# Five accumulation tiles and three tiles for transposes, instead of six and two, in layer 1's query, key and value stage

## The chip, the cores and the metric

One core of a Trainium2 chip runs the whole program. The metric is the device time of one execution in microseconds, the median of three runs. A profile of one further execution gives the time line of each engine: TensorE (PE; its weight loads are listed as PEld), VectorE (DVE), ScalarE (ACT), GpSimd (POOL) and the DMA queue that SyncE (SP) issues.

## What is computed

The reference is a model of two layers over 2048 tokens and 256 context tokens of width 1024, in float32. Layer 0 is a mixer of convolutions and a state space scan; layer 1 is attention with low-rank projections, 16 heads and a query and key width of 96 (64 without and 32 with rotary positions). The change lies in the part that makes layer 1's queries, keys and values:

```
cq, ckv, kr, gate = jnp.split(h @ w_in, cuts, axis=-1)          # widths 384, 256, 32, 1024
q  = (rms_norm(cq, q_a_norm) @ w_uq).reshape(b_, n, 16, 96)
kv = (rms_norm(ckv, kv_a_norm) @ w_ukv).reshape(b_, n, 16, 64 + 64)
q_nope, q_rope = rms_norm(q[..., :64], ...), rms_norm(q[..., 64:], ...)
k_nope, v, k_rope = rms_norm(kv[..., :64], ...), kv[..., 64:], rms_norm(kr, ...)
q_rope, k_rope = apply_rope(q_rope, cos, sin), apply_rope(k_rope, cos, sin)
```

## The kernel before

Float32 products are made in float32 precision from three matmuls (high by high, high by low, low by high; lines 120 to 122 in `mm3`). The stage works on 18 tiles of 128 tokens: tiles 0 and 1 are context (no queries), 2 to 17 are the tokens. For each tile there are these steps, and the names below are those of the code:

- `b_in(n)`: the down projection, one PSUM tile `pk` (288 columns, 24 matmuls) and one `pq` (384 columns, 24 matmuls). ScalarE squares both for the norms (L1382 to L1388).
- `b_r3(n)`: the three reciprocal square roots of a tile, a chain of small VectorE operations (L1397, L1398, L127 to L135).
- `b_cn(n)`: scales and writes the normed row `cn`; it is the last reader of `pk` and `pq` (ScalarE L1405 and L1410, VectorE L1407).
- `b_tr(n)`: two tiles of transposes of `cn` (L1430 to L1448).
- `b_up(n)`: four accumulation tiles for keys and values (512 columns, 6 matmuls each, L1468 to L1470 empty them, the last reader is VectorE's L1470) and four for queries (384 columns, 9 matmuls each, emptied by ScalarE's L1498), then the norms of all heads on VectorE (`k_scale`, the chain rB) and the scaling on GpSimd (L1483, L1509 to L1521).
- `b_heads(n)`: five tiles of four transposes (`evacT`, L1527), each emptied by ScalarE (L1541 or L1538) and then VectorE (L1542 or L1539) and stored by a DMA.

All accumulation tiles come from one PSUM pool (`accB`) and all transposes from another (`tpB`); together the two pools hold eight tiles. A buffer is handed out again once the last instruction that reads it is done, so a later tile's first matmul waits for that instruction. The first three tiles are put in order by a scheduler. From there on the order is that of the code, written out in `weave`: while tile n has just been through `b_in`, tile n-1 is projected up and the heads of tile n-2 are transposed, in turns:

```
for x_ in range(9):
    next(up, None)              # b_up(n-1): accumulation tile x_ (4 for keys and values, 4 for queries)
    if x_ < 2:
        drive(r3, 2)            # b_r3(n)
    if x_ == 2:
        run_all(r3)
        if n:
            b_cn(n)
    if x_ >= wait:
        next(hd_, None)         # b_heads(n-2): one tile of transposes
```

`weave` runs for n = 3 to 17 with such a `b_cn`, fifteen times; after each of them come `b_tr(n)` and `b_in(n+1)`. In what follows kv0 to kv3 are the four tiles for keys and values of a turn, uq0 to uq3 those for queries, and T3 to T7 the five tiles of head transposes. On TensorE the turn reads kv0, kv1, T3, kv2, T4, kv3, T5, uq0, T6, uq1, T7, uq2, uq3, then the two tiles of `b_tr` (T1, T2), pk, pq. `pk` and `pq` of tile n are open from before kv0 until `b_cn(n)`, which stands on the other engines behind kv2 and T3. Every engine runs its own queue in order.

The stage begins at about 1256 us and ends at about 1711 us of the span. Attention over the 16 heads follows until the end.

Of the kernel before, what the change touches and what calls it, by code (L numbers as in the profile page):

```python
# [17 lines left out]
PSUM = bass.MemoryType.PSUM  # L18
# [39 lines left out]
def hybrid_conv_s5_mla_kernel(tc, x, c, ctx, c_ctx, mod_w, mod_b, norm_w, e_w_in, e_conv_w, e_lam_re, e_lam_im,  # L58
# [11 lines left out]
    with ExitStack() as top:  # L70
# [177 lines left out]
        with ExitStack() as l0:  # L248
# [5 lines left out]
            acc_p = psum.enter_context(tc.tile_pool(name="acc0", bufs=3, space=PSUM))  # L254
# [518 lines left out]
            acc_p = psum.enter_context(tc.tile_pool(name="acc", bufs=6, space=PSUM))  # L773
# [81 lines left out]
            acc_p = psum.enter_context(tc.tile_pool(name="acc1", bufs=4, space=PSUM))  # L855
# [218 lines left out]
            acc_p = glu_psum.enter_context(tc.tile_pool(name="acc2", bufs=6, space=PSUM))  # L1074
# [81 lines left out]
        with pa:  # L1156
            acc_p = pa.enter_context(tc.tile_pool(name="accA", bufs=6, space=PSUM))
            tp_p = pa.enter_context(tc.tile_pool(name="tpA", bufs=2, space=PSUM))
# [160 lines left out]

        man = ExitStack()  # L1320
        with ExitStack() as pb:
            acc_p = pb.enter_context(tc.tile_pool(name="accB", bufs=6, space=PSUM))
            tp_p = pb.enter_context(tc.tile_pool(name="tpB", bufs=2, space=PSUM))
            wt0 = pb.enter_context(tc.tile_pool(name="wB0", bufs=1))
            wt = pb.enter_context(tc.tile_pool(name="wB", bufs=1))

# [944 lines left out]
```

## Time and profile before

| what | us |
|---|---|
| median of 3 runs | 3494.16 (3493.05 to 3504.32) |
| the profiled execution, its own time | 3490.75 |
| span of the profiled execution | 3489.0 |
| TensorE busy in the span | 3222.4 (92%) |
| VectorE, ScalarE, GpSimd busy | 2605.1, 2174.0, 2130.2 |
| mean granted TensorE clock | 0.97 |

The span is the time from the first to the last instruction. [...] In a timeline the bracket at the end of a row gives how long the engine was idle before that instruction, and which instruction on another engine ended the wait.

### The profile page before, as it was taken

To read this page: it belongs to the slowest core of one execution; us is meant where nothing else is said; L and a number is where in the kernel's file an instruction comes from. 1 tells how busy PE (TensorE), PEld (TensorE's weight loads), DVE (VectorE), ACT (ScalarE), POOL (GpSimd) and SP (SyncE) were. 2 spreads that over 40 slices of the span, in tenths; PEclk is the share of its full clock that TensorE was granted. 3 is DMA by queue.
4 is the path that set the end of the run, shared out by engine and by line. 5 is a ranking of instruction groups with operands and counts; after the bars stand their busy time and mean duration, and the time that the engine had idled before them with its cause. 6 is when DMAs were issued, how large, how long until landed. Compare 5 with 4: busy or idle time off the path is not lost.

```text
span 3489.0 us, 63902 instructions
## 1 busy us (share of the span) xinstructions
PE 3222.4 (92%) x24725; PEld 2685.1 (77%) x24725; DVE 2605.1 (75%) x3958; ACT 2174.0 (62%) x2873; POOL 2130.2 (61%) x1331
## 2 busy tenths in 40 slices
PE   5998999989889888888799999999999999999997
PEld 4876877767778678888677777777788878788776
DVE  5766327484267676666688888899889988888897
ACT  4211322121334354444599998899999999999995
POOL 2455022222375323333378988898889988889886
PEclk9998999999999899999899999999999999999998
DMA  7333856654576657766845445555447665576783
GB/s 198 123 104 99 270 146 177 169 159 135 166 239 226 202 134 160 166 157 161 200 137 159 139 128 166 165 172 156 145 134 217 186 186 149 156 235 185 235 237 134
DMA packets 503646, 594.26 MB, mean 170 GB/s; under 512 B 85235, under 2 KB 355016, under 8 KB 495280
## 3 DMA queue, kind: packets, MB, share of 16 engines
q1 hardware_dynamic: 492208, 573.34, 57.7%
q0 software_dynamic: 2688, 8.46, 0.7%
q10 hardware_dynamic: 8448, 8.39, 0.7%
q8 instruction: 196, 3.21, 0.4%
q14 instruction: 106, 0.87, 0.1%
HBM read 394.95 MB, written 195.13 MB: 169 GB/s over the span
## 4 chain that ended last, share of the span: by engine, by line
PE 56%; DVE 14%; POOL 13%; issue 6%; DMA 5%; ACT 4%; SPq 1%; POOLq 0%; ACTq 0%; DVEq 0%
PE accps L320 11%; POOL pl L2021 8%; PE O L2041 7%; PE s L120 5%; PE s L121 5%; PE s L122 5%; PE fps L120 2%; PE fps L122 2%; PE fps L121 2%; PE s5ps L967 2%; POOL ph L2013 2%; PE accA L121 2%; PE accA L122 2%; PE accA L120 2%; PE accB L122 1%
## 5 line engine op out<-in xcount | busy, mean ns | idle before, releaser
L2021 POOL TENSOR_TENSOR pl<-S,ph 128x1024 f16<-128x1024 f32 x430 | 918.9, 2161 | 11.2 <-ACT ph L2015 10.5
L2000 DVE TENSOR_TENSOR S<-S,t 128x1024 f32<-128x1024 f32 x432 | 520.4, 1212 | 35.7 <-PE t L1995 35.3
L2005 ACT ACTIVATE S<-S,psh 128x1024 f32<-128x1024 f32 x432 | 498.6, 1154 | 54.2 <-DVE S L2000 53.3
L1971 DVE TENSOR_TENSOR rm<-s,rm 128x1024 f32<-128x1024 f32 x384 | 468.5, 1220 | 74.9 <-ACT S L1959 55.1
L320 PE MATMUL accps<-aT,wh 128*128 128x480 f32 (+2 forms) x1920 | 490.6, 386 | 5.2 <-ACT wh L114 3.3
L120 PE MATMUL s<-q,K 96*128 96x512 f32 x1134 | 465.1, 410 | 19.3 <-DVE rm L1971 13.0
L1959 ACT COPY S<-s 128x1024 f32<-128x1024 f32 x432 | 434.5, 1006 | 41.7 <-PE s L122 29.3
L121 PE MATMUL s<-q,K 96*128 96x512 f32 x1134 | 446.1, 393 | 0.0
L122 PE MATMUL s<-q,K 96*128 96x512 f32 x1134 | 445.9, 393 | 0.0
L2041 PE MATMUL O<-Vy,ph 128*128 128x129 f16 (+2 forms) x5760 | 437.0, 210 | 0.0
L320 PEld LDWEIGHTS accps<-aT,wh 128*128 128x128 f32 x1920 | 342.4, 193 | 69.6 <-issue 17.8
L2041 PE MATMUL O<-Vy,pl 128*128 128x65 f16 x4608 | 335.5, 195 | 25.5 <-POOL pl L2021 17.2
L2041 PEld LDWEIGHTS <-pl 128*128 128x128 f16 x4608 | 240.6, 98 | 149.0 <-issue 82.3
L2015 ACT CAST ph<-S 128x1024 f16<-128x1024 f32 x288 | 302.3, 1050 | 23.4 <-PE O L2041 20.3
L2021 POOL TENSOR_TENSOR pl<-Sy,ph 128x1024 f16<-128x1024 f32 x142 | 305.5, 2171 | 8.0 <-DVE ph L2011 4.2
L2041 PEld LDWEIGHTS <-ph 128*128 128x128 f16 x5760 | 286.8, 98 | 0.0
L320 PE MATMUL accps<-aT,wl 128*128 128x480 f32 (+2 forms) x960 | 267.1, 376 | 8.7 <-POOL wl L117 8.7
L120 PEld LDWEIGHTS s<-q,K 96*128 96x128 f32 x1134 | 213.8, 189 | 71.8 <-DVE rm L1971 15.6
L122 PEld LDWEIGHTS s<-q,K 96*128 96x128 f32 x1134 | 213.2, 188 | 47.9
L121 PEld LDWEIGHTS s<-q,K 96*128 96x128 f32 x1134 | 215.0, 190 | 40.4
L117 POOL TENSOR_TENSOR wl<-w,wh 128x1024 fp32r<-128x1024 f32 x25 | 61.7, 2470 | 257.5 <-ACT wh L114 237.2
L320 PEld LDWEIGHTS accps<-aT,wl 128*128 128x128 f32 x960 | 176.5, 193 | 38.0 <-POOL wl L117 10.0
(504 smaller groups left out, 7237.5 us busy)
## 6 DMA issues: line engine op xcount, KB each, us to landing
at<-a1d SPq DMA_DIRECT2D x47, 1024.0 KB
K<-kd SPq DMA_DIRECT2D x101, 384.0 KB
w<-in_e_w_in_dram SPq DMA_DIRECT2D x48, 512.0 KB
at<-atd SPq DMA_DIRECT2D x48, 512.0 KB
Vy<-vd SPq DMA_DIRECT2D x34, 580.5 KB
K<-krd SPq DMA_DIRECT2D x101, 192.0 KB
mw<-in_mod_w_dram SPq DMA_DIRECT2D x64, 256.0 KB
a1d<-at SPq DMA_DIRECT2D x16, 1024.0 KB
```

What stands on the lines that cost most here:

```text
L120: PE.matmul(ps, lh, rh, start=start, stop=False)
L121: PE.matmul(ps, lh, rl, start=False, stop=False)
L122: PE.matmul(ps, ll, rh, start=False, stop=stop)
L320: PE.matmul(a_[:, 0:(j1 - j0) * q], lw[:, k, :], rt[:, k, j0 * q:j1 * q], start=(k == 0 and lw is wh and rt is aT[0]), stop=(k == KD - 1 a ...
L967: PE.matmul(o, l_, r_, start=e + n == 0, stop=e + n == 4, skip_group_check=True)
L1959: S.copy(out=st["S", p], in_=st["ps", p])
L1971: V.tensor_tensor(out=rm, in0=ps, in1=st["S", 0] if p == 1 else rm, op=ALU.max)
L2000: V.tensor_tensor(out=sb, in0=sb, in1=state[i]["mb"][:, None, :].to_broadcast([P, 2, 512]), op=ALU.subtract)
L2005: S.activation(out=sb, in_=sb, func=AF.Exp, scale=scale, bias=psh[:, 0:1])
L2015: S.copy(out=st["ph", p], in_=st["S", p])
L2021: e.tensor_tensor(out=st["pl", p], in0=st["S", p], in1=st["ph", p], op=ALU.subtract)
L2041: PE.matmul(part(r_, v.shape[-1]), w[:, a, r_ * P:(r_ + 1) * P], v, start=(c_ == 0 and n == 0), stop=(c_ == 17 and n == 8), skip_group_che ...
```

## The change

The stage's eight PSUM tiles are divided differently: five for accumulation and three for transposes. Nothing else is edited.

```diff
-            acc_p = pb.enter_context(tc.tile_pool(name="accB", bufs=6, space=PSUM))
-            tp_p = pb.enter_context(tc.tile_pool(name="tpB", bufs=2, space=PSUM))
+            acc_p = pb.enter_context(tc.tile_pool(name="accB", bufs=5, space=PSUM))
+            tp_p = pb.enter_context(tc.tile_pool(name="tpB", bufs=3, space=PSUM))
```

On VectorE, ScalarE, GpSimd and SyncE the order of the instructions is the same as before. On TensorE it differs at one place alone, in the part that the scheduler orders: the pq of tile 3 (`accB<-K`) and the first transposes of `b_tr(0)` (`tpB<-idf,cnA`).

```order
 L121 MATMUL accB<-v_8224,at 128x288
 L122 MATMUL accB<-t_8221,at 128x288
-L120 MATMUL accB<-K,at 128x384
-L121 MATMUL accB<-K,at 128x384
-L122 MATMUL accB<-K,at 128x384
 L1430 MATMUL tpB<-idf,cnA 128x128 x2
 L1431 MATMUL tpB<-idf,cnA 32x128
```

The transposes now stand ahead of three matmuls that they followed.

What differs in each turn of `weave` is what an instruction waits for. The next two pieces show TensorE, with the semaphores that a row waits for in brackets (DVE, Activation and Pool are the counters of VectorE, ScalarE and GpSimd). The first begins at T4 (`tpB<-idf,Sy`) and ends in kv3 (`accB<-kvh,ckA`).

```order
-L1527 MATMUL tpB<-idf,Sy 128x128 [waits DVE_49]
+L1527 MATMUL tpB<-idf,Sy 128x128 [waits DVE_49,PE_49]
 L1527 MATMUL tpB<-idf,Sy 128x128 x3
-L120 MATMUL accB<-kvh,ckA 128x512
+L120 MATMUL accB<-kvh,ckA 128x512 [waits DVE_49]
 L121 MATMUL accB<-kvl,ckA 128x512
 L122 MATMUL accB<-kvh,ckA 128x512
```

kv3 waits for VectorE now and did not wait before. Counting VectorE's instructions up to the value waited for, the one meant is L1470 of kv0.

The second is T5 and the head of uq0 (`accB<-uqh,cqA`).

```order
-L1527 MATMUL tpB<-idf,Sy 128x128 [waits DVE_49,Pool_49]
+L1527 MATMUL tpB<-idf,Sy 128x128 [waits Pool_49]
 L1527 MATMUL tpB<-idf,Sy 128x128 x3
-L120 MATMUL accB<-uqh,cqA 128x384 [waits Activation_49]
+L120 MATMUL accB<-uqh,cqA 128x384 [waits DVE_49]
 L121 MATMUL accB<-uql,cqA 128x384
 L122 MATMUL accB<-uqh,cqA 128x384
```

T5 no longer waits for VectorE (before, for L1542 of T3); uq0 waits for VectorE instead of ScalarE, by the same count for L1470 of kv1. By that count T6 waits for L1542 of T3 (before, of T4), uq1 for L1410 of `b_cn`, and T7 for L1542 of T4 (before, of T5); uq2 and uq3 wait for nothing further.

## Rows read from the trace of the kernel before

**Rows 1.** The head of the page: span and number of instructions.

```profile
span 3489.0 us, 63902 instructions
```

**Rows 2.** Chain of waits, TensorE's own, 1300 to 1700 us: total, times, longest.

```profile
PE tpB L1527 <- DVE tT L1542: 25.7, 8, 3.3
...
PE tpB L1527 <- DVE u L1542: 22.2, 7, 3.2
```

**Rows 3.** Windows by token tile: us, busy PE, PEld, DVE, ACT, POOL, clock, DMA.

```profile
1301.50:1328.20 26.70, 23.19 (x126) 21.59 (x125) 16.56 (x51) 12.73 (x32) 7.27 (x6) 0.87 0.78 180
...
1407.50:1434.40 26.90, 23.70 (x137) 22.06 (x135) 17.46 (x51) 13.06 (x33) 8.72 (x8) 0.94 0.69 160
...
1461.40:1486.70 25.30, 22.13 (x137) 20.54 (x135) 17.45 (x51) 12.88 (x33) 8.71 (x8) 1.00 0.72 170
...
1673.80:1700.00 26.20, 20.08 (x92) 17.27 (x91) 17.41 (x51) 13.56 (x32) 8.71 (x8) 0.87 0.88 195
```

**Rows 4.** Timeline of one tile, TensorE: start, length, line, tiles, [idle before].

```profile
1407.39 0.48 PE L120 MATMUL accB<-kvh,ckA 128*128 128x512 f32 x1
...
1412.21 0.63 PE L1527 MATMUL tpB<-idf,Sy 128*128 128x128 f32 x4 [3.20 <-DVE u L1542]
...
1412.60 0.42 PE L120 MATMUL accB<-uqh,cqA 128*128 128x384 f32 x1
...
1417.84 0.60 PE L1527 MATMUL tpB<-idf,Sy 128*128 128x128 f32 x4
...
1418.19 0.42 PE L120 MATMUL accB<-uqh,cqA 128*128 128x384 f32 x1
...
1421.40 0.38 PE L1430 MATMUL tpB<-idf,cnA 128*128 128x128 f32 x2
```

**Rows 5.** Timeline of the same tile, VectorE, and of the next tile's start.

```profile
1404.74 0.42 DVE L1470 TENSOR_TENSOR Vy<-accB,Vy 128x256 f16<-128x256 f32 x1 [3.05 <-ACT Vy L1469]
...
1409.32 0.42 DVE L1470 TENSOR_TENSOR Vy<-accB,Vy 128x256 f16<-128x256 f32 x1
...
1411.32 0.75 DVE L1542 SCALAR_TENSOR_TENSOR u<-tpB,cols,u 128x512 fp32r<-128x512 f32 x1
...
1412.32 0.24 DVE L1407 SCALAR_TENSOR_TENSOR cnA<-accB,r3y,wr 128x32 f32<-128x32 f32 x1
...
1413.24 0.74 DVE L1542 SCALAR_TENSOR_TENSOR tT<-tpB,cols,tT 128x512 fp32r<-128x512 f32 x1
...
1431.72 0.42 DVE L1470 TENSOR_TENSOR Vy<-accB,Vy 128x256 f16<-128x256 f32 x1 [3.06 <-ACT Vy L1469]
```

**Rows 6.** Timeline of the same tile, ScalarE.

```profile
1411.79 0.57 ACT L1410 ACTIVATE cnA<-accB,r3y 128x384 f32<-128x384 f32 x1
...
1419.30 0.57 ACT L1538 CAST u<-tpB 128x512 fp32r<-128x512 f32 x1
```

**Rows 7.** Timeline of the stage's first tiles, TensorE and VectorE.

```profile
1293.00 0.40 PE L120 MATMUL accB<-kvh,ckA 128*128 128x512 f32 x1
...
1294.12 0.75 DVE L1470 TENSOR_TENSOR Vy<-accB,Vy 128x256 f16<-128x256 f32 x2
...
1308.23 1.08 PE L1527 MATMUL tpB<-idf,Sy 128*128 128x128 f32 x4 [3.33 <-DVE tT L1542]
```

**Rows 8.** Timeline of the last such tile, SyncE's queue and ScalarE.

```profile
1680.90 1.90 SPq L103 DMA_DIRECT2D wg<-in_o_w_in_dram  x2
...
1686.77 0.63 ACT L114 CAST t<-wg 128x512 fp32r<-128x512 f32 x1
```

**Rows 9.** Timeline of TensorE after the stage: two short gaps.

```profile
1727.04 0.47 PE L120 MATMUL s<-K 96*128 96x512 f32 x1 [1.23 <-DVE rm L1971]
...
1737.09 0.47 PE L120 MATMUL s<-K 96*128 96x512 f32 x1 [1.51 <-DVE rm L1971]
```

**Rows 10.** Windows of 2 us behind each of those gaps, columns as in Rows 3.

```profile
1728.00:1730.00 2.00, 2.00 (x12) 1.65 (x11) 0.83 (x2) 0.86 (x2) 0.00 (x0) 1.00 0.97 258
...
1738.00:1740.00 2.00, 2.00 (x6) 1.51 (x6) 0.38 (x1) 0.28 (x1) 0.00 (x0) 0.50 1.18 323
```

## The prediction

> **What bounds the kernel now.** The profiled execution took 3490.75 us, of which 3489.0 are the span [rows 1]; that is 3.4 below the median of the runs, 3494.16. The change touches one stage, 1256 to 1711 us; the stage behind it waits for its last keys and queries, so what the stage gains or loses is gained or lost at the end. I read first the chain of waits of TensorE for the stage's middle. It has next to nothing but one line: the head transposes, L1527, waited 15 times for VectorE's L1542, 8 + 7 times, 25.7 + 22.2 us together, 3.2 us each time [rows 2]. Fifteen is the number of turns of `weave` that carry a `b_cn`. Then the windows, one per turn. TensorE is busy for 23.7 of 26.9 us, and the rest is that one stall, while VectorE is busy for 17.5 and ScalarE for 13 [rows 3]. So TensorE runs without pause except there, and a turn is as long as its work plus the stall.
>
> The same table shows a second cost. Of its 15 windows three are 25.3 to 25.4 us long at a granted clock of 1.00, and ten (all others but the first and the last) are 26.9 or 27.0 us at 0.94 [rows 3]. The stall is the same in both kinds. [...]
>
> The timeline of one turn shows what the stall hangs on. kv3 starts at 1407.39; T5 starts at 1412.21 after 3.20 us of idleness [rows 4]. It needs the buffer of T3, since only two exist, and T3's last reader is the L1542 that VectorE begins at 1411.32 and ends at 1412.07 [rows 5]. T3 itself was long in PSUM: VectorE had in front of that L1542 the chain of `b_r3`, between the L1470 of kv0 at 1404.74 and that of kv1 at 1409.32, and its remainder behind it [rows 5].
>
> **The change part by part.** Instructions are neither added nor removed. With three buffers T5 finds a free one. Its data, written by GpSimd's L1509, is ready long before, so it starts when kv3 is issued: TensorE stopped at 1412.21 - 3.20 = 1409.01. T5 costs 1418.19 - 1417.84 = 0.35 us at full clock, a query tile (1421.40 - 1418.19) / 2 = 1.60 [rows 4].
>
> With five accumulation tiles, two of which are pk and pq until `b_cn`, the others turn among three. kv3 waits for the L1470 of kv0, done at 1404.74 + 0.42 = 1405.16 [rows 5], 2.2 us ahead of kv3's start at 1407.39 [rows 4]: no cost. uq0 waits for the L1470 of kv1, done at 1409.74 [rows 5], where T5 ends about 1409.4: a new stall of some 0.4 us. uq0 then runs from 1409.8 to 1411.4. T6 now waits for the release that T5 waited for, L1542 of T3, and so starts when T5 used to, at 1412.21: a second stall, of 0.8 us. uq1 needs L1410 of `b_cn`, done at 1411.79 + 0.57 = 1412.36 [rows 6], while T6 runs to 1412.56: free. T7 needs L1542 of T4, done at 1413.24 + 0.74 = 1413.98 [rows 5], against 1412.56 + 1.60 = 1414.16: free by 0.2. The rest of the turn has no wait that the change moves. So exactly T5 and uq0 move into the old stall: 0.35 + 1.60 = **1.95 us per turn**, and 3.2 us of idleness become two pieces of 0.4 to 0.8.
>
> Does the work behind it keep up? ScalarE empties T5, uq0, T6, uq1, T7, uq2 sooner after each other; about 3.6 us of work stand between `b_cn` and uq3's copy, which it can finish within 0.3 us of uq3's end. If it is late, VectorE has 3.06 us of idleness ahead of the next turn's first L1470 as cover [rows 5]. T7 goes into the store buffer of T3, whose DMA must have ended. ScalarE's L1538 for T7 ran at 1419.30 [rows 6] with no wait for a DMA and would now run near 1416.7. The trace does not show when the store landed. At best it costs nothing; at worst it lands just before 1419.30, 2.6 us late, of which the cover above takes most: I take nothing and allow 0.6 us per turn, 8 us in all. DMA is busy for 0.69 to 0.72 of a turn [rows 3], 18.6 of 26.9 us, and fits into 23.4.
>
> **The clock.** Whether the short stalls still make it fall no row of this stage shows. After the stage a gap of 1.23 us left the clock at 1.00, one of 1.51 us was followed by 0.50 [rows 9, 10]; and the 3.2 us stall spared it in three of thirteen turns [rows 3]. The new pieces, 0.4 and 0.8, are nearer to the first, so I take it that the clock stays, and that all ten turns get their 1.6 us back.
>
> The sum: 13 x 1.95 = 25.4, and 10 x 1.6 = 16.0. The first turn (n = 3) has a stall of 3.33 us [rows 7] and a clock of 0.87 [rows 3] to give back, but the tiles before it lose: a kv3 that ran at 1293.00 now waits for an L1470 done at about 1294.54 behind another VectorE chain [rows 7], 1.5 us, and the next tiles wait likewise. Its gain lies between 0 and 3.33 + 1.6 = 4.9; I take 3, nearer the upper end since the lost time partly falls into the old stall. In the last turn (n = 17) ScalarE also splits the gates' weights, L114 at 1686.77, from a load issued at 1680.90 [rows 8]; 3.55 us earlier that load may not be there. Between 0 and 1.95 + 1.6; I take 2. Together **46.4 us**: 3494.2 - 46.4 = 3448 in terms of the median, and a turn of 23.4 us.
>
> **The rivals.**
>
> *The clock falls in every turn all the same.* For it: the 1.51 us gap [rows 9, 10], and 0.4 + 0.8 come within 3 us of each other. Against it: the 3.2 us in one piece was spared three times. Then ten turns gain 1.95, three gain 1.95 - 1.6 = 0.35, and the two at the ends 2 together: 19.5 + 1.1 + 2 = 22.6, so 3472.
> [...]
>
> *The wait only changes its name.* If uq0 were given pk's buffer it would wait for L1407, done at 1412.56 [rows 5], and start at 1412.6 as before [rows 4]. Only T5's 0.35 us is won, 13 x 0.35 = 4.6: 3490. The order of the releases speaks against it: pk is the last freed, not the first.
>
> *The shortage of accumulation tiles is worse than that of transposes.* This decides if the five buffers are handed out strictly in turn: then kv3, not uq0, gets pk's buffer and waits until 1412.56 [rows 5], and kv3 and T5, about 1.4 + 0.35 us, run after the stall where before they ran ahead of it or in it. uq0 comes 1.75 us later in each turn, 13 x 1.75 = 22.8, and a stall of 5 us lowers the clock in the three spared turns too, 4.8: 3522. Against it stands the count of VectorE's instructions, which gives L1470 of kv0 for kv3.
>
> **How the numbers follow.** My forecast 0.80, the clock 0.10, the changed name 0.04, the shortage 0.06. About 0.3%, 10.5 us, is what a measurement of this kernel can tell from no change. Forecast and clock rival are faster by more: 0.90; same 0.04; slower 0.06. The forecast's own range: the two end turns can give 4.7 more or 5 less, late copies cost up to 8, the runs differ by some 4 us: 3438 to 3463. The clock rival at 3472 is taken in, with 1 us, and 2 below for runs like the profiled one: 3436 to 3473.
>
> **What would show it.** Right: the wait of L1527 for L1542 falls from 3.2 to about 0.8 us and moves to T6, a wait of uq0's L120 for L1470 of 0.4 us appears, windows per turn are 23.4 us at clock 1.00. The clock rival: the same waits, 25.0 us at 0.93. Wrong altogether: kv3 waits for L1407, or uq0 starts at L1407's end as before.

## The result, and the profile after

| | before | after |
|---|---|---|
| runs of the prediction's comparison, us | 3494.16, 3493.05, 3504.32, 3499.92 | 3460.72, 3444.06, 3448.74, 3455.76 |
| median, us | 3497.04 | 3452.25 |
| ratio | | 0.9872, 95% interval 0.9848 to 0.9896 |

The changed kernel is 44.8 us faster than before (1.3%; 36 to 53 us by the interval). Forecast were 46.4 us, 3448 against 3494. The profiled execution of the changed kernel, 3460.72 us, is the slowest of its four.

The head of its page, which answers to [rows 1]:

```profile
span 3458.9 us, 63899 instructions
```

The three instructions fewer are semaphore instructions of TensorE; every engine does as many operations as before.

The chain of waits of TensorE, 1300 to 1650 us, which answers to [rows 2]: line, what it waited for, total, times, longest.

```profile
PE accB L120 <- DVE Vy L1470: 6.2, 16, 1.1
PE tpB L1527 <- DVE u L1542: 3.4, 7, 0.5
PE tpB L1527 <- DVE tT L1542: 3.4, 7, 0.5
PE accB L120 <- ACT ckA L1434: 3.2, 1, 3.2
```

The fifteen waits of 3.2 us have become fourteen of 0.5, and the accumulation tiles, which had next to none, have waits of 6.2 us in sixteen pieces. The last row is the stage's last turn, told below.

Windows from one L1397 (the first operation of `b_r3`) to the next, columns as in [rows 3]. The first begins with n = 4, the second is a turn of the middle, the third goes from n = 17 to the first scores.

```profile
1327.34:1350.53 23.19, 22.46 (x135) 20.61 (x134) 17.38 (x51) 12.71 (x32) 8.50 (x7) 1.00 0.78 172
...
1397.15:1420.47 23.32, 22.51 (x136) 20.64 (x135) 17.52 (x52) 12.71 (x32) 8.77 (x7) 1.00 0.81 186
1630.35:1665.38 35.03, 29.60 (x156) 25.75 (x155) 23.86 (x61) 20.52 (x46) 16.59 (x14) 0.90 0.84 180
```

All thirteen turns n = 4 to 16 are 23.2 to 23.4 us long at a granted clock of 1.00 (a share of full speed). Before, ten were 26.9 to 27.0 us at 0.94 and three 25.4 us at 1.00 [rows 3].

The timeline of TensorE in that turn answers to [rows 4]: T4, kv3, T5, uq0, T6, uq1, T7, uq2, and the first of `b_tr`.

```profile
1399.10 0.60 PE L1527 MATMUL tpB<-idf,Sy 128*128 128x128 f32 x4
1399.45 0.48 PE L120 MATMUL accB<-kvh,ckA 128*128 128x512 f32 x1
...
1400.93 0.60 PE L1527 MATMUL tpB<-idf,Sy 128*128 128x128 f32 x4
...
1401.85 0.44 PE L120 MATMUL accB<-uqh,cqA 128*128 128x384 f32 x1 [0.32 <-DVE Vy L1470]
...
1404.17 0.66 PE L1527 MATMUL tpB<-idf,Sy 128*128 128x128 f32 x4 [0.49 <-DVE u L1542]
1404.59 0.42 PE L120 MATMUL accB<-uqh,cqA 128*128 128x384 f32 x1
...
1406.24 0.60 PE L1527 MATMUL tpB<-idf,Sy 128*128 128x128 f32 x4
1406.59 0.42 PE L120 MATMUL accB<-uqh,cqA 128*128 128x384 f32 x1
...
1409.81 0.38 PE L1430 MATMUL tpB<-idf,cnA 128*128 128x128 f32 x2
```

T5 follows kv3 without a pause, uq0 waits 0.32 us for the L1470 of kv1, T6 waits 0.49 us for the L1542 of T3, and nothing else stands. Two stalls of 0.8 us together have taken the place of one of 3.2.

Where the time went is read from four marks, the stage's first matmul (1248.91 us in the kernel before), the L1397 of n = 4, the L1397 of n = 17, and the first scores behind it (1707.50). The kernels of the experiments are in the table too; their tiles are given as accumulation and transposes.

| kernel | first matmul to n = 4 | n = 4 to n = 17 | n = 17 to scores | stage | gain |
|---|---|---|---|---|---|
| before (6 and 2) | 76.8 | 345.7 | 36.1 | 458.6 | |
| after (5 and 3) | 73.4 | 303.0 | 35.0 | 411.5 | 47.1 |
| 5 and 2 | 74.4 | 346.7 | 36.0 | 457.1 | 1.5 |
| 4 and 4 | 84.2 | 333.7 | 33.1 | 451.0 | 7.6 |
| 6 and 2, 17 matmuls in the stall | 72.5 | 329.8 | 34.4 | 436.8 | 21.8 |
| 6 and 2, 8 matmuls in the stall | 76.9 | 329.8 | 33.0 | 439.7 | 18.9 |
| 6 and 2, rope later, first try | 75.1 | 356.3 | 35.0 | 466.4 | -7.9 |
| 6 and 2, rope later, second try | 72.5 | 292.2 | 31.4 | 396.0 | 62.6 |
| 5 and 3, rope later, second try | 72.9 | 287.1 | 30.9 | 390.9 | 67.7 |

The stage gives 47.1 us: 3.4 in the first tiles, 42.7 in the thirteen turns, 1.0 at the end. The profiled execution as a whole gains only 30.1 us (3489.0 - 3458.9), because two pieces that hold the same instructions in both kernels went the other way in it: the stage began 5.0 us later (1253.91 against 1248.91), and the part behind the stage took 1793.5 us against 1781.5. The profiles of the other runs, below, show that the second is spread between executions of one kernel, and that the stage is not; the later start may belong to the program.

### The profile page after: what moved, and what is told of

Read it like the earlier page. It is cut to its first block, busy times and chain, and to the rows that moved or that the text cites. A ratio compares the mean times of both kernels' runs of the same rounds, so it can differ in the third digit from the quotient of the medians.

```text
span 3458.9 us, 63899 instructions
## 1 busy us (share of the span) xinstructions
PE 3216.8 (93%) x24725; PEld 2671.6 (77%) x24725; DVE 2613.1 (76%) x3958; ACT 2169.1 (63%) x2873; POOL 2129.0 (62%) x1331
## 4 chain that ended last, share of the span: by engine, by line
PE 31%; POOL 12%; DVE 8%; issue 5%; ACT 5%; DMA 1%; POOLq 0%; SPq 0%; ACTq 0%; DVEq 0%
POOL pl L2021 8%; PE O L2041 8%; PE s L120 5%; PE s L122 5%; PE s L121 5%; PE fps L120 2%; PE fps L122 2%; PE fps L121 2%; POOL ph L2013 2%; POOL Sy L1509 1%; DVE raw L1735 1%; DVE rm L1971 1%; POOL Sy L1483 1%; PE fps L1981 1%; ACT S L1959 1%
## 5 line engine op out<-in xcount | busy, mean ns | idle before, releaser
L120 PE MATMUL s<-q,K 96*128 96x512 f32 x1134 | 466.4, 411 | 24.9 <-DVE rm L1971 18.6
```

Source lines behind the costliest of these rows:

```text
L120: PE.matmul(ps, lh, rh, start=start, stop=False)
```

## The experiments

The medians of the kernel before differ by some 12 us between the groups of runs (3497 to 3509), so every kernel is held against the runs of before made beside it, and a difference in us is the ratio less one, times that median (the ratios are not exactly the quotients of the medians beside them).

### Half of the change: five accumulation tiles, two for transposes

```diff
-            acc_p = pb.enter_context(tc.tile_pool(name="accB", bufs=6, space=PSUM))
+            acc_p = pb.enter_context(tc.tile_pool(name="accB", bufs=5, space=PSUM))
```

> Half of the change: five accumulation tiles, still two for transposes. Theory (the third transposes buffer is what brings the time): T5 goes on waiting for VectorE's L1542 of T3, 3.2 us in each turn, ten of the turns n = 4 to 16 stay at 26.9 us with the clock at 0.94; only the first tiles change. About 3495, between 3489 and 3502. Rival (the fewer accumulation tiles, or tile 3's pq standing behind b_tr(0) as in the change, bring part of it): below 3480.

Measured: 3509.74 us against 3505.26, ratio 1.0003 (0.9984 to 1.0022). A turn of this kernel from the windows, and its chain of waits of TensorE, 1330 to 1640 us:

```profile
1407.02:1433.95 26.93, 23.77 (x136) 22.12 (x135) 17.49 (x52) 13.12 (x32) 8.77 (x7) 0.94 0.70 161
```

```profile
PE tpB L1527 <- DVE tT L1542: 19.2, 6, 3.3
PE tpB L1527 <- DVE u L1542: 19.0, 6, 3.2
```

The stall and the turns are those of before. Beside two buffers for transposes the sixth accumulation tile was worth nothing, and the gain is the third transposes buffer's.

### Work in the stall, with the stall's cause left in place

Seventeen or eight matmuls without use stand ahead of T5 and write into the tile that uq0 will begin from zero.

```diff
                     if n == 3:
                         dma(out=vd[:, :, kt, :].rearrange("h p n -> p h n"), in_=vt)
+                        if 3 <= kt < 17:
+                            early.append(accB()[:, 0:384])
+                            for _ in range(17):
+                                PE.matmul(early[0], ck[:, 0, 0], kvh[:, 0, 0:384], start=True, stop=True)
...
-                    ps = accB()[:, 0:384]
+                    ps = early.pop() if early else accB()[:, 0:384]
```

> The kernel before, with 17 matmuls of 128x384 without use (0.178 us each by the nine of a query tile in 1.60 us, 3.0 us together) behind kv3 in the fourteen turns n = 4 to 17, so that TensorE has work where it stood; T5 waits for L1542 as before. Theory (the fall of the clock is a cost of its own, 1.6 us in each of ten turns, and goes when TensorE does not stand): all turns 25.3 to 25.4 us at a granted clock of 1.00 with 0.2 to 0.3 us of stall left, 16 to 18 us faster than before, about 3479. Rival (the clock column only goes with something else, or the extra work itself lowers the clock): turns of 26.9 us, 3490 to 3500.

> As the run with 17 matmuls, but with 8 (1.4 us), which leaves a stall of 1.8 us in front of T5. If a stall of this size still lowers the clock, as the 1.51 us gap after the stage did: turns of 26.9 us in most places, 3490 to 3498. If the clock stays as it does behind stalls of 0.3 to 0.5 us in the changed kernel: turns of 25.3 us, about 3479. In between if it falls in some of the turns, as the 3.2 us stall did.

Measured: with 17, 3486.11 us against 3505.26, ratio 0.9938 (0.9918 to 0.9958), 21.7 us faster; with 8, 3489.15 us, ratio 0.9949 (0.9930 to 0.9968), 17.9 us faster. One turn of each from the windows, and the rest of the stall in the timeline of the kernel with 8 (there L1532 is the head transposes and L1547 is L1542):

```profile
1421.73:1447.09 25.36, 25.20 (x153) 23.62 (x152) 17.50 (x51) 12.93 (x32) 8.78 (x7) 1.00 0.71 155
```

```profile
1426.45:1451.81 25.36, 23.61 (x144) 22.03 (x143) 17.51 (x51) 12.92 (x32) 8.78 (x7) 1.00 0.75 168
...
1433.56 0.63 PE L1532 MATMUL tpB<-idf,Sy 128*128 128x128 f32 x4 [1.75 <-DVE tT L1547]
```

Extra work made the kernel faster. All thirteen turns of both kernels are 25.35 to 25.5 us at a clock of 1.00: T5 comes no sooner than before, but the 1.6 us of a lowered clock are gone from ten of them, 345.7 - 329.8 = 15.9 us. That is the second term of the prediction by itself, forecast at 16.0. The 4.3 us that the run with 17 has in the first tiles are chance: no matmuls were added there, and the clock happened to stay at 1.00 in the turn n = 3 (23.28 us), behind the same 3.3 us stall that the kernel before has there at 0.87 (26.06 us); with 8 the first tiles took 76.9 us, as before. Another 1.7 to 3.1 us come at the end. The run with 8 says more: with 1.75 to 1.9 us of stall left the clock stayed at 1.00 in every turn. So the changed kernel, with its 0.3 and 0.5, had room to spare if stalls are compared by their length.

### One step further: four and four

```diff
-            acc_p = pb.enter_context(tc.tile_pool(name="accB", bufs=6, space=PSUM))
-            tp_p = pb.enter_context(tc.tile_pool(name="tpB", bufs=2, space=PSUM))
+            acc_p = pb.enter_context(tc.tile_pool(name="accB", bufs=4, space=PSUM))
+            tp_p = pb.enter_context(tc.tile_pool(name="tpB", bufs=4, space=PSUM))
```

> One step further: four accumulation tiles and four for transposes. Two accumulation tiles then turn beside pk and pq. By the count of the semaphores kv3 now waits for L1470 of kv1, which in the changed kernel ends at 1401.79 where kv3 would start at 1399.45: a stall of 2.3 us; uq0 waits for L1410 (1404.42) where T5 would end at 1403.55: 0.9 us; the stall of T6 goes. The turn is 1.7 to 1.8 us longer than in the changed kernel, 25.0 to 25.1 us at clock 1.00 (the 2.3 us are between the 1.8 us behind which the clock stayed and the 3.2 us behind which it mostly fell; if it falls, 26.6 us): 20 to 25 us faster than before, or 0 to 5 if the clock falls. Rival (a fourth buffer for transposes helps as the third did, accumulation is not short): 23.3 us or less.

Measured: 3500.22 us against 3508.72, ratio 0.9983 (0.9966 to 0.9999), 6 us faster than before and some 39 slower than the changed kernel. Two neighbouring turns from the windows, and the chain of waits of TensorE, 1330 to 1640 us:

```profile
1435.38:1461.46 26.08, 23.96 (x136) 22.03 (x135) 17.47 (x51) 13.01 (x32) 8.74 (x7) 0.93 0.72 163
1461.46:1486.63 25.17, 22.53 (x136) 20.74 (x135) 17.49 (x52) 12.90 (x32) 8.74 (x7) 1.00 0.74 171
```

```profile
PE accB L120 <- DVE Vy L1470: 25.6, 12, 2.3
PE accB L120 <- ACT cnA L1410: 3.1, 6, 0.5
```

The forecast stall of kv3 is there, 2.1 to 2.3 us in each turn; uq0's is 0.5 us in every second turn instead of 0.9 in each. A turn at full clock is 25.17 us (25.0 to 25.1 expected). The open point, the clock, came out in between: it falls in every second turn. What was not in the expectation is the loss in the first tiles, 84.2 us against 76.8: accumulation tiles wait there for L1470 by up to 2.8 us each, and the first transposes 5.2 us for L1405. So the shortage of accumulation tiles that the prediction named as a rival exists; it begins at four, not at five.

### Why was L1542 of T3 late at all?

The prediction took the late L1542 as it stood: VectorE had the chain of `b_r3` ahead of it. In the changed kernel's trace that chain is odd. These are its three longest operations, of three columns each, and beside them the operations that GpSimd ran at the time (start and length):

```profile
1397.34 1.17 DVE L1398 TENSOR_SCALAR ss<-ss 128x3 f32<-128x3 f32 x1
...
1398.75 1.14 DVE L129 TENSOR_SCALAR r3y<-r3t 128x3 int32<-128x3 int32 x1
...
1400.12 1.14 DVE L134 SCALAR_TENSOR_TENSOR r3t<-r3t,ss 128x3 f32<-128x3 f32 x1
...
1402.49 0.16 DVE L134 SCALAR_TENSOR_TENSOR r3t<-r3t,ss 128x3 f32<-128x3 f32 x1
```

```profile
1397.19 1.29 POOL L1519 TENSOR_TENSOR Sy<-Sy,rqB 128x512 f32<-128x512 f32 x1
1398.56 1.30 POOL L1520 TENSOR_TENSOR Sy<-Sy,rqB 128x512 f32<-128x512 f32 x1
1399.94 1.29 POOL L1521 TENSOR_TENSOR Sy<-Sy 128x512 f32<-128x512 f32 x1
```

L1398 ends at 1398.51, L129 at 1399.89, L134 at 1401.26; L1519 ends at 1398.48, L1520 at 1399.86, L1521 at 1401.23. Each of the three ends 0.03 us behind one rope operation of GpSimd, and the same L134 takes 0.16 us once GpSimd is done. In the kernel before the same three take 1.19, 1.14 and 1.14 us, beside the same three operations of GpSimd. The three hold VectorE for about 3.0 us longer than they need, nearly the whole of the 3.2 us stall. The first try moves the three rope operations behind `b_cn`: GpSimd is given one of `b_cn`'s small products (L1414), which needs L1407, and the rope operations (in a function `rope`, put aside in a list) stand behind it in GpSimd's queue.

```diff
-                    V.tensor_tensor(out=ro[:, 0], in0=krv, in1=rt[:, 0], op=ALU.mult)
+                    (GP if kt > 2 else V).tensor_tensor(out=ro[:, 0], in0=krv, in1=rt[:, 0], op=ALU.mult)
...
-                er.tensor_tensor(out=qa, in0=qr[:, :, ::-1, :], in1=rq[:, 1][:, None].to_broadcast(sh_), op=ALU.mult)
-                er.tensor_tensor(out=qr, in0=qr, in1=rq[:, 0][:, None].to_broadcast(sh_), op=ALU.mult)
-                er.tensor_tensor(out=qr, in0=qr, in1=qa, op=ALU.add)
...
+                late.append(rope)
+                if kt == 17:
+                    late.pop()()
...
                         if n:
                             b_cn(n)
+                        if late:
+                            late.pop()()
```

> The kernel before with six and two tiles; the last three of GpSimd's four rope operations (L1519 to L1521, 1.3 us each) are moved behind b_cn of the next tile, by giving GpSimd L1414, which needs L1407, ahead of them. Theory (the small VectorE operations of b_r3 that take 1.1 to 1.2 us, where others of the same size take 0.17, last until the rope operation then running on GpSimd ends, and this is what makes L1542 of T3 late): the three held operations fall to about 0.2 us, L1542 of T3 comes 3 us earlier, the stall in front of T5 falls from 3.2 to at most 0.3 us, turns are 22.3 to 22.8 us at clock 1.00: 10 x 4.4 + 3 x 2.8 + 3 for the end turns = 55 us faster, about 3440, below the changed kernel. Rival (the chain is slow by itself or waits for ScalarE): the operations stay at 1.1 us, the stall at 3.2 us, about 3494. Second rival (rope is then late for T7): the wait goes to T7 and for GpSimd, 1 to 3 us per turn, 3455 to 3480.

Measured: 3512.88 us against 3505.26, ratio 1.0015 (0.9999 to 1.0032): not faster. The theory held for the chain and the plan failed behind it. The timeline of TensorE and VectorE in one turn (L1533 the head transposes, L1548 is L1542; L1399 is L1398, L1417 to L1421 the small operations of `b_cn`):

```profile
1407.93 0.17 DVE L1399 TENSOR_SCALAR ss<-ss 128x3 f32<-128x3 f32 x1
...
1412.62 1.27 DVE L1417 TENSOR_TENSOR cnA<-roA 128x32 f32<-128x32 f32 x1 [0.15 <-POOL roA L1415]
1415.22 0.19 DVE L1420 TENSOR_TENSOR rqB<-rtA,wr 128x32 f32<-128x32 f32 x1 [1.32 <-POOL Sy L1523]
1415.33 1.25 DVE L1421 TENSOR_TENSOR rqB<-rtA,wr 128x32 f32<-128x32 f32 x1
1416.51 0.74 DVE L1548 SCALAR_TENSOR_TENSOR tT<-tpB,cols,tT 128x512 fp32r<-128x512 f32 x1
```

```profile
1411.91 0.63 PE L1533 MATMUL tpB<-idf,Sy 128*128 128x128 f32 x4 [0.23 <-DVE u L1548]
...
1417.30 0.66 PE L1533 MATMUL tpB<-idf,Sy 128*128 128x128 f32 x4 [3.19 <-DVE tT L1548]
```

`b_r3` runs in 0.15 to 0.17 us per operation now, and T5 waits 0.23 us in place of 3.2. But the rope operations now run while VectorE does the small operations of `b_cn`, and hold L1417 for 1.27 us and L1421 for 1.25. Between them L1420 waits 1.32 us for something else: it writes a buffer of `rqB` that the rope operation still reads, because rope comes a turn later now and `rqB` has two buffers. The L1542 of T4 comes behind all this, and T6 waits 3.19 us for it. The stall had moved by one tile, and a turn was 27.3 to 27.5 us, at a clock of 0.94 in all thirteen.

The second try mends these points: VectorE's two products for `rqB` stand first and the last operation of `b_cn` is GpSimd's, so that all of VectorE's are done when rope begins, `rqB` has three buffers, and T7, which needs rope's result, stands behind uq2. The edit is against the kernel before; the part with `rope` is as above.

```diff
+                    rq = wk.tile([P, 2, 2, ROPE // 2], F32, name="rqB", bufs=3)
...
-                    V.tensor_tensor(out=krv, in0=ro[:, 0], in1=ro[:, 1], op=ALU.add)
...
-                    rq = wk.tile([P, 2, 2, ROPE // 2], F32, name="rqB")
...
+                    (GP if kt > 2 else V).tensor_tensor(out=krv, in0=ro[:, 0], in1=ro[:, 1], op=ALU.add)
...
-                    if x_ >= wait:
+                    if x_ >= wait and not (n and n > 3 and x_ == 5):
```

It ran with six and two tiles, with five and three, and beside the changed kernel itself.

> Six and two tiles. GpSimd's last three rope operations behind b_cn as in the run before, with what that run lacked: the last of b_cn's small operations (the sum that ends the key's rotation) is the one given to GpSimd, VectorE's other four stand ahead of it, rqB has three buffers in place of two, and T7 stands behind uq2 in place of uq1. Theory (small VectorE operations wait for GpSimd's operation to end; nothing else made L1542 of T3 late): no VectorE operation of 128x3 or 128x32 takes over 0.3 us, neither T5 nor T6 stalls by more than 0.3 us, turns of 22.2 to 22.7 us at clock 1.00, 55 to 60 us faster than before and 10 to 14 faster than the changed kernel, with the old division of PSUM. Rival (two buffers for transposes stay short even so): stalls of 1 us or more somewhere in T5 to T7 or T1, T2; turns of 23.3 us or more, no better than the changed kernel.

> The same with five and three tiles. Theory: with the late L1542 gone the third buffer has nothing left to hide: the same turns of 22.2 to 22.7 us and within 4 us of the run with six and two. Rival (the third buffer has a worth of its own): turns at least 0.3 us shorter than with six and two, 4 us or more in all.

> The changed kernel once more, on the chip of the three others of this call, so that they can be compared with it. Theory: 45 to 47 us faster than before (ratio 0.987), turns n = 4 to 16 of 23.3 us at clock 1.00 with 0.3 and 0.5 us of stall.

Measured against 3508.72 us: the changed kernel 3462.98, ratio 0.9872 (0.9848 to 0.9896); rope later with six and two 3448.96, ratio 0.9842 (0.9814 to 0.9870); rope later with five and three 3447.70, ratio 0.9822 (0.9797 to 0.9846). One turn from the windows of each of the last two, six and two first, then, from another turn with six and two, operations of VectorE beside those of GpSimd:

```profile
1456.38:1478.80 22.42, 22.19 (x136) 20.61 (x135) 14.54 (x51) 13.00 (x32) 9.01 (x9) 1.00 0.84 193
```

```profile
1463.74:1485.76 22.02, 22.02 (x136) 20.62 (x135) 14.54 (x50) 12.99 (x32) 8.98 (x9) 1.00 0.86 196
```

```profile
1434.15 0.17 DVE L1399 TENSOR_SCALAR ss<-ss 128x3 f32<-128x3 f32 x1
...
1438.69 0.19 DVE L1420 TENSOR_TENSOR roA<-cnA,rtA 128x32 f32<-128x32 f32 x1
...
1441.52 0.75 DVE L1548 SCALAR_TENSOR_TENSOR tT<-tpB,cols,tT 128x512 fp32r<-128x512 f32 x1 [0.22 <-ACT tT L1547]
```

```profile
1439.17 1.31 POOL L1522 TENSOR_TENSOR Sy<-Sy,rqB 128x512 f32<-128x512 f32 x1
1440.56 1.30 POOL L1523 TENSOR_TENSOR Sy<-Sy,rqB 128x512 f32<-128x512 f32 x1
```

L1399, held for 1.17 us in the changed kernel (there L1398), takes 0.17; the small operations of `b_cn` are done before rope begins. VectorE is listed as busy for 14.5 us of a turn in place of 17.5: of the 3.0 us, at most 0.2 are the sum that GpSimd has now, and the rest was time in which VectorE stood behind GpSimd, which the profile counts as busy. With the old division of PSUM the turn falls to 22.4 us, below the 23.3 of the changed kernel; T5 waits 0.23 us in place of 3.2, in two of the thirteen turns 0.6, which was not expected. So nearly all of the shortage of buffers for transposes came from VectorE being held, and the third buffer covers a delay whose cause lies between VectorE and GpSimd. (T7's later place also relieves those buffers; its share was not measured apart, but T5's wait was down to 0.23 us in the first try, without it.) Once that is removed the third buffer is still worth the last 0.4 us of a turn (22.42 to 22.02 us: TensorE then does not stand at all), 5.1 us of the stage; that is the rival's figure, if a small one. In whole runs the two can't be told apart, their intervals overlap. Both medians are below that of the changed kernel in this group, by 14 and 15 us; the interval of the one with five and three lies wholly below the changed kernel's, that of the other overlaps it a little. Five and three with rope later is faster than the kernel before and than the changed kernel.

### What lies outside the stage

> The kernel before once more, for one look at what lies outside the stage. In its first profile the stage's first matmul starts at 1248.91 us; in the two profiles of the changed kernel at 1253.91 and 1254.58, though the instructions ahead of it are the same in number and order. If that belongs to each program, it starts here between 1248 and 1250 again; if it is spread between runs, anywhere from 1247 to 1258. The part behind the stage (first scores to end) was 1781.5 us in the first profile and 1790 to 1802 in those of all other kernels: by the same two readings 1779 to 1784, or up to 1802.

> The changed kernel a third time, beside it. If the start of the stage belongs to the program: 1253 to 1256 us, and 1793 to 1798 us from the first scores to the end; if it is spread, 1247 to 1258 and 1780 to 1802. The stage between them 410 to 412 us by both.

Single runs, 3510.70 and 3469.93 us; a further one of the kernel before beside them took 3496.92. In the profile of the kernel before the part behind the stage took 1798.4 us (1781.5 in the first profile), so that part is spread between executions of one kernel, and the first profile of before was a quick one. The stage itself took 458.0 us (458.6 before). The three profiles of the changed kernel have 411.5, 410.7 and 411.4 us, and the rest took 1793.5 to 1802.7.

The start of the stage came out by neither reading. In the kernel before it was at 1252.47 us (1248.91 before), so it moves by 3.6 us. But over all twelve profiles the kernels do not mix: it lies at 1247.7 to 1252.5 us in the eight with two or four buffers for transposes, and at 1253.9 to 1257.9 in the four with three. They are apart long before the stage: one and the same matmul of TensorE, some 720 us ahead of it, starts at 525.8 to 528.2 us in the eight and at 530.7 to 533.5 in the four. Why stays open. If it belongs to those programs, the change loses some 5 us ahead of the stage out of the 47.1 that it gains in it; the 44.8 us of the runs, with an interval of 36 to 53, leave both open.

## Why the prediction was right

By its own steps:

- **The new waits.** Forecast were uq0 behind the L1470 of kv1 by 0.4 us and T6 behind the L1542 of T3 by 0.8; the rows have 0.32 and 0.49, and no wait of T7. Both stalls are smaller because the last matmul ahead of a pause is listed as busy to its end (T5 for 0.60 us, where 0.35 lie between T7 and uq2); from T5's start to T6's, 1412.21 - 1409.01 = 3.20 us were forecast and 3.24 passed. T5 itself starts 1.48 us behind kv3's start, where the prediction took the listed end of kv3, 1.62. The turn was to be 23.4 us and is 23.3.
- **1.95 us per turn** from T5 and uq0 in the old stall: in the turns that had the full clock before, it is 25.36 - 23.31 = 2.05. The kernels that only fill the stall give the term for all thirteen turns: 329.8 - 303.0 = 26.8 us, where 25.4 were forecast.
- **Ten times 1.6 us of clock.** The 1.6 us are 26.95 - 25.35, the lengths of the ten turns at 0.94 and of the three at 1.00 [rows 3]. In the turn of [rows 4] the matmuls of the query tiles start 0.32 us apart from 1413.22 to 1414.82, and 0.17 us apart again from 1416.62 on. The term is shown apart from the rest by the kernels that only fill the stall: 15.9 us. The step that no row of before could settle, whether short stalls leave the clock alone, was taken right, and not narrowly: the clock was 1.00 in all thirteen turns with stalls of 0.32 and 0.49 us, and in all thirteen with one of 1.75 to 1.9. Its ground was weaker than its outcome. The 1.51 us gap after the stage that it counted as a danger was the third within some eleven us (behind 1.23 and 1.17); the 1.75 us, longer and alone in their turn, left the clock at 1.00. The rival that the clock falls all the same is not borne out for this pattern of two short stalls: the windows of the thirteen turns are at 1.00 throughout.

```profile
1413.54 0.52 PE L121 MATMUL accB<-uql,cqA 128*128 128x384 f32 x1
1413.86 0.52 PE L122 MATMUL accB<-uqh,cqA 128*128 128x384 f32 x1
1414.18 0.52 PE L120 MATMUL accB<-uqh,cqA 128*128 128x384 f32 x1
...
1416.79 0.34 PE L120 MATMUL accB<-uqh,cqA 128*128 128x384 f32 x1
1416.97 0.34 PE L121 MATMUL accB<-uql,cqA 128*128 128x384 f32 x1
1417.14 0.34 PE L122 MATMUL accB<-uqh,cqA 128*128 128x384 f32 x1
```

- **The first tiles**, 3 us, gave 3.4, and that they agree so well is luck. 1.3 of the 3.4 is the time between the first two tiles' L1397, 2.16 us before and 0.89 after, which lies anywhere between 0.5 and 2.2 in the twelve profiles. The change itself did two things. The tiles of the beginning lose as forecast: a kv3 waits 1.44 us, later tiles 0.66 and 1.14, and the time from tile 2's L1397 to tile 3's grows from 21.67 to 23.49 us. The turn n = 3 wins: the 3.33 us stall is gone, and it falls from 26.06 us at a clock of 0.87 to 22.00 at 1.00. Together that is 2.2 us; against the run with 17 matmuls in the stall, in which the clock stayed at 1.00 in the same turn (23.28 us), it would have been a loss of 0.5.

```profile
1298.95 0.50 PE L120 MATMUL accB<-kvh,ckA 128*128 128x512 f32 x1 [1.44 <-DVE Vy L1470]
...
1305.48 0.50 PE L120 MATMUL accB<-kvh,ckA 128*128 128x512 f32 x1 [0.66 <-DVE Vy L1470]
...
1308.72 0.44 PE L120 MATMUL accB<-uqh,cqA 128*128 128x384 f32 x1 [1.14 <-DVE Vy L1470]
```

- **The last turn**, 2 us, gave 1.0 (-0.4 to 1.9 between the other profiles of the two kernels); this term was too large, and for the reason named: the load of the gates' weights is not there yet.

```profile
1644.35 0.62 ACT L114 CAST t<-wg 128x512 fp32r<-128x512 f32 x1 [1.45 <-DMA wg<-in_o_w_in_dram]
...
1647.05 0.50 PE L120 MATMUL accB<-kvh,ckA 128*128 128x512 f32 x1 [3.23 <-ACT ckA L1434]
```

ScalarE waits 1.45 us for it, its L1434 is late, and kv0 of tile 17 waits 3.23 us for that (1.56 in the kernel before).

- **Late copies and stores**, nothing taken and 8 us allowed: the thirteen turns show no wait of ScalarE or VectorE for a DMA.
- **The other rivals.** In the thirteen turns uq0 did not get pk's buffer, and kv3 waited for nothing. The shortage of accumulation tiles has its place one step further, with four. That a stall of 5 us would lower the clock in every turn, 4.8 us of that rival's sum, was an estimate from the 3.2 us that did so in ten of thirteen; no run has such a stall in these turns.

The sum was 46.4 us, the stage gives 47.1, and the runs 44.8 with an interval that holds both. The ends of the range have a slip: by the bounds given, the two end turns could give 1.9 + 1.55 = 3.45 us more, not 4.7, and the losses add up to 3465, not 3463; the result lies far inside either. What the prediction did not see is why the L1542 was late. It named VectorE's chain as work, where three of its operations were a wait for GpSimd. The forecast for this change did not hang on it; a forecast of what else could be done would have.

## What to carry to other kernels

When a buffer shortage stalls an engine, look first at why its last reader is late: here a third buffer won 45 us, and moving three operations of another engine, with what that needed, won 55 with the old buffers. Price a stall by what comes with it as well: of these 3.2 us one third of the gain was the clock that fell behind them (15.9 of 47.1 us in the stage), and even useless work in the stall was a gain (17.9 and 21.7 us). Buffers taken from another pool are free until the count of tiles in use says they are not: five were enough, four cost back nearly all.

## What the runs showed of the hardware

**Small VectorE operations lasted until a GpSimd operation beside them ended, and were shown as busy all that time.** Operations of 128x3 (L1398, L129, L134) that take 0.16 to 0.17 us took 1.14 to 1.19 in the kernels before and after, and those of the changed kernel end 0.03 us behind GpSimd's; operations of 128x32 that take 0.19 took 1.27 and 1.25 (rope later, first try). Not every VectorE operation did so: an L1542 (listed as L1548, rope later, second try, six and two), which reads PSUM, that began at 1441.52 in the midst of the rope operation of 1440.56 to 1441.86 kept its 0.75 us. What decides which of them is held no run here shows.

**The clock and the length of a stall.** One stall per turn of 1.75 to 1.9 us, in the kernel with 8 matmuls in the stall, left the granted clock at 1.00 in thirteen of thirteen turns; one of 2.1 to 2.3, in the kernel with four and four, lowered it in every second turn (0.93 in those); one of 3.2 in ten or eleven of thirteen (0.94; three profiles with two buffers for transposes), and in the first try with rope later, where it stands one tile further on, in all thirteen (0.94). So it was in this stage's turns of 25 to 27.5 us, with TensorE otherwise busy; the runs show no rule behind it.
